# Tokens' 1/rms applied behind the input products instead of to x, seven products on two pairs of the first block, and a later fetch of x by tokens

## The chip, the cores and the metric

The kernel runs on one core of one Trainium2 chip. The metric is the device time of one launch in microseconds (us), as a median over runs; the trace is of one more execution, taken by the hardware profiler.

## The reference, cut to what matters

x has 256 tokens of 2,048 values, all in float32. h is x divided by its root mean square per token, times a gain norm_g. h times a matrix of 2,048 x 11,264 gives nine parts: q, k, v, the gate z_a (1,024 columns each), u_b, v_b, z_b (1,024 each) and g_a, g_b (2,048 each).

```python
h = rms_norm(x, norm_g)
proj = h @ w_in
q, k, v, z_a, u_b, v_b, z_b, g_a, g_b = jnp.split(proj, cuts, axis=-1)
q = rms_norm(q per head, q_norm_g); k = rms_norm(k per head, k_norm_g)
y_a = (attention(q, k, v) * silu(z_a)) @ w_proj_a
sgu = gelu(u_b) * (W_s @ rms_norm(gelu(v_b)) + b)
y_b = (sgu * silu(z_b)) @ w_proj_b
out = x + (sigmoid(g_a) * y_a + sigmoid(g_b) * y_b) @ w_out
```

The 1/rms of a token is one factor of a whole row of proj, so it can be applied to x or to the rows of proj.

## The kernel before, in words

**Precision.** Each float32 operand is split into a high half (a cast to float32r by ScalarE, names ending in h) and a low half (the difference, by VectorE, names ending in l). A product is three matmuls, lo x hi, hi x hi and hi x lo (three(), L298 to L303), each 128x128 by 128x512.

**The weight stream.** schedule() (L50) lists 120 groups; each is 1 MB of weights, fetched on SyncE's queue (load, L116) into one of four rotating buffers "raw". For an input or output block of 1,024 columns ("quad": q, k, v, za, vb, ub, zb, four g, two out) a group is one pair kp of k tiles: tile kp and tile kp + 8 of the 2,048 rows, that is a 2x2 block product. It is done in one of two ways:
- plain (direct(), L307): 8 block products, 24 matmuls into four accumulators; the weights need one cast of 2,048 columns (L125) and one difference (L126);
- seven products (seven(), L321): Strassen's scheme in Winograd's form, 21 matmuls into seven banks; the weights need combinations t (L143, L145, L146), casts whp (L152) and th (L154), differences wlp (L155) and tl (L157). t stands in a buffer of the raw rotation. The x side needs four combinations of the blocks of x, "forms" (L277 and L282), with their halves Fh and Fl (L291). At the end of the block early() (L346, a copy on ScalarE and four operations on VectorE) and final() (four more) combine the seven banks.

Pairs 0 to 3 of a block (and 4 of g) take the seven products, the others the plain way. The first block, q, is plain throughout: groups 0 to 7, pairs 0 to 7 in that order (PLAIN, L46).

**x in the first block.** xT holds x by channels, in the order of the pairs; load_x (L171) fetches k tiles p0 to p1 of it, so load_x(2, 4) is pair 1. The first piece, xv, has the small vectors and tile 0. split_x (L201) multiplies a pair by norm_g and makes the halves xuh and xul; q is computed with these, x not yet divided by its rms. Meanwhile x by tokens, xnat, is fetched (two 1 MB pieces, L187 to L190, around the fourth weight group), stats (L241) sums its squares on ScalarE, GpSimd takes the power -0.5, two transposes spread 1/rms along the free axis (stats_row, L246), VectorE multiplies x by it (normalise, L254), and halves_x (L258) makes the halves xh and xl, with which all later blocks work. q's four accumulators are copied out with 1/rms as ScalarE's scale (L690).

**The order.** Each engine runs its instructions in one order. For ScalarE and VectorE the code before L659 and the first eight passes of the loop (L658) stand inside manual_schedule (L634, closed at L660): their instructions keep the written order. In pass i the loop issues load(i + 3), split(i + 2) and split_x, then the matmuls of group i, then what at() (L572, L581 on) has put down for group i. The other engines' orders, TensorE's and the DMA queue of SyncE among them, are the scheduler's, which also may put a later instruction into a gap.

**Pools.** "big" has ten slots of 1 MB (xt0, xt1, xnat0, xnat1, xuh, xul, xh, xl, the forms and later tiles), "unit" ten of 256 KB, "raw" four, wh and wl three each, whp and wlp two each. PSUM has eight banks; a block's seven products use four banks E beside its four accumulators L, and the next block swaps the two sets. The vector gain of the spatial part (L230) is a constant tile, the spatial weights ws (L227) stand in "unit"; both are fetched by load_mix (L223), put down for the fifth block.

**After the products.** sums (L370) takes the squares of q, k and v_b per head on ScalarE, and GpSimd's power gives rs (rsqrt, L236); norm_qk and norm_v multiply by rs; func applies Silu or Gelu; turn_p (L454) transposes the attention weights and copies them out of PSUM.

Of the kernel before, what the change touches and what calls it, by code (L numbers as in the profile page):

```python
# [44 lines left out]
OUT = ((0, 1, 4, 2, 5, 3, 6, 7), (4, 0, 1, 5, 2, 3, 6, 7))  # L45
PLAIN = (0, 1, 2, 3, 4, 5, 6, 7)  # L46
NVEC = KT + 2 + H


def schedule():  # L50
    s = []

    def quad(name, c, order):
        s.extend(("quad", name, c, kp, n) for n, kp in enumerate(order))

    quad("q", 0, PLAIN)
    for name in ("k", "v", "za", "vb", "ub", "zb"):
        quad(name, 0, MIXED)
    for c in range(4):
        quad("g", c, GATE)  # L60
        s.extend(("proj", "proj", c, q, q) for q in range(4))
    for c in range(2):
        quad("out", c, OUT[c])
    return s
# [3 lines left out]
def hybrid_layer_kernel(  # L68
# [26 lines left out]
    def bank(b, name):  # L95
        return psum.tile([P, B], F32, tag=f"b{b}", name=name)
# [8 lines left out]
    def strassen(i):  # L105
        if i >= NG or G[i][0] != "quad" or G[i][1] == G[0][1]:
            return False
        return G[i][3] in SK or (G[i][1] == "g" and G[i][3] == 4)

# [71 lines left out]
    load_x(2, 4)  # L181
    load(1, pieces=2)
    load_x(4, 8)
    load(2, pieces=2)
    load_x(8, 12)
    load_x(12, 16)
    xn = [slot(F32, f"xnat{m}") for m in range(2)]  # L187
    nc.sync.dma_start(xn[0], x[0:P, :])
    load(3)
    nc.sync.dma_start(xn[1], x[P:S, :])  # L190
    for i in range(2):
# [40 lines left out]
    rstd = const.tile([P, 2], F32, name="rstd")  # L232
    R = xv[:, NVEC:]
    ssum = const.tile([P, 2], F32, name="ssum")
# [6 lines left out]
    def stats():  # L241
        for m in range(2):
            nc.scalar.activation(xn[m], xn[m], AF.Square, accum_out=ssum[:, m:m + 1])
        rsqrt(rstd, ssum, 2, D)

    def stats_row():  # L246
        ps = bank(0, "ps_R")
        for m in range(2):
            nc.tensor.transpose(ps[:, m * P:(m + 1) * P], rstd[:, m:m + 1].to_broadcast([P, P]), ident)
        nc.scalar.copy(R, ps[:, 0:S])  # L250

    xh, xl = [None, None], [None, None]

    def normalise(i):  # L254
        src = xt[i]
        nc.vector.tensor_tensor(src, src, R[:, None, :].to_broadcast([P, 8, S]), op=ALU.mult)

    def halves_x(i):  # L258
        xh[i] = slot(F32R, f"xh{i}").rearrange("p (k t) -> p k t", t=S)
        xl[i] = slot(F32R, f"xl{i}").rearrange("p (k t) -> p k t", t=S)  # L260
        nc.scalar.copy(xh[i], xt[i])
        nc.vector.tensor_tensor(xl[i], xt[i], f(xh[i]), op=ALU.subtract)

# [9 lines left out]
    def halves_4():  # L273
        nc.scalar.copy(spare(xh[0]), X["F4"])
        nc.vector.tensor_tensor(spare(xl[0]), X["F4"], f(spare(xh[0])), op=ALU.subtract)

# [92 lines left out]

    def sums(C, name):  # L370
        for m in range(2):
            for c in range(2):
                ss = small.tile([P, 4], F32, tag="ss", bufs=8, name="ss")
                junk = u("junk")
                for h in range(4):
                    nc.scalar.activation(junk[:, h * P:(h + 1) * P], C[m][c][:, h * P:(h + 1) * P], AF.Square,
                                         accum_out=ss[:, h:h + 1])
                rs = small.tile([P, 4], F32, tag="rs", bufs=8, name="rs")
                rsqrt(rs, ss, 4, P)
                X["rs", name, m, c] = rs  # L380

# [18 lines left out]
    def func(name, fn):  # L400
        for m in range(2):
            for c in range(2):
                nc.scalar.activation(X[name][m][c], X[name][m][c], fn)

# [49 lines left out]
    def turn_p(hg, banks):  # L454
        pt = X["PT", hg] = slot(F32, f"PT{hg}")[:, 0:12 * P].rearrange("p (n h t) -> p n h t", n=3, t=P)
        for n, (c, b) in enumerate(((0, 0), (1, 0), (1, 1))):
            s = X["S0", hg] if c == 0 else X["S1"][:, 4 * hg:4 * hg + 4, :]
            ps = bank(banks[n], f"ps_p{hg}{n}")
            for h in range(4):
                nc.tensor.transpose(ps[:, h * P:(h + 1) * P], s[:, h, b * P:(b + 1) * P], ident)  # L460
            nc.scalar.copy(pt[:, n], ps.rearrange("p (h t) -> p h t", t=P))

# [117 lines left out]

    i0 = first["q", 0]  # L581
    at(i0 + 1, stats)
    at(i0 + 3, stats_row)
    at(i0 + 3, normalise, 1)
    at(i0 + 4, halves_x, 1)
    at(i0 + 5, normalise, 0)
    at(i0 + 4, forms_4)
    at(i0 + 5, lambda: forms(xt[0], "x"))
    at(i0 + 6, halves_x, 0)
    at(i0 + 6, halves_f, "x")  # L590
    at(i0 + 20, halves_4)
# [48 lines left out]
    split(0, 4, [3])  # L640
    for kp in range(1, 4):
        split_x(kp)
        if kp < 2:
            split(kp, 4)
    def fac(name):
        if name == "q":
            return xu_h, xu_l
        if name == "out":
            return [X.get(("mh", i)) for i in range(2)], [X.get(("ml", i)) for i in range(2)]
        return xh, xl  # L650

# [6 lines left out]
    for i, (kind, name, c, kp, n) in enumerate(G):  # L658
        if i == 8:  # L659
            ordered.close()  # L660
        if i:
            load(i + 3)
        split(i + 2, 2 if i == 0 else 1)
        if i < 4:
            split_x(i + 4)
        plain = i < 8
        if kind == "quad":
            if n == 0:
# [4 lines left out]
                Et = None  # L673
            if len(Lt) == 3 and (plain or not strassen(i)):
                Lt.append(bank(L[3], f"acc_{name}{c}_3"))
            if strassen(i) and Et is None:
                Et = [bank(b, f"seven_{name}{c}_{j}") for j, b in enumerate(E)]
            if strassen(i):
                last = 4 if name == "g" else SK[-1]
                f8 = "m" if name == "out" else "x"  # L680
                seven(Et, Lt, i, kp, kp == SK[0], kp == last, n > 0, *fac(name), X["Fh", f8], X["Fl", f8])
                if kp == last:
                    e = early(Et, f"{name}{c}", xres.get(c) if name == "out" else None)
            else:
                direct(Lt, *fac(name), i, kp, (n == 0, not direct22(i)), n == 7)
            if n == 7:
                if plain:
                    X[name] = [[u(f"{name}{m}{j}") for j in range(2)] for m in range(2)]
                    for j in range(4):
                        nc.scalar.activation(X[name][j // 2][j % 2], Lt[j], AF.Copy, scale=rstd[:, j // 2:j // 2 + 1])  # L690
                elif name == "out":
                    post_out(c, Lt, e)
                elif name == "g":
                    X["g", c] = final(Lt, e)
                    for m in range(2):
                        for j in range(2):
                            nc.scalar.activation(X["g", c][m][j], X["g", c][m][j], AF.Sigmoid)
                else:
                    X[name] = final(Lt, e)
# [79 lines left out]
```

## Time and profile before

| | us |
|---|---|
| median of the three runs | 672.03 |
| lowest and highest | 668.34, 673.25 |
| the profiled execution, device time | 668.8 |
| its span in the trace | 667.0 |

Times in the trace are microseconds from the start of the span, durations in the page's groups nanoseconds. PE is TensorE's matmul row, PEld its weight loads, DVE VectorE, ACT ScalarE, POOL GpSimd, SP SyncE; SPq is a sequencer issuing a DMA. In the timeline a matmul's own duration (0.39 us) is longer than the step from one matmul to the next, since matmuls overlap; the starts are what counts. A bracket at the end of a line says how long the engine stood idle before it and what ended that.

### The profile page before, as it was taken

Reading aid. Unit: us, or ns where it says so; the run is one execution under the profiler, and the core shown is the slowest. Engines: PE = TensorE matmul, PEld = TensorE weight load, DVE = VectorE, ACT = ScalarE, POOL = GpSimd, SP = SyncE. Lnnn points to the kernel's source line nnn. Section 1 sums busy time; section 2 is a strip of 40 time slices with the busy share of each in tenths; the row PEclk is TensorE's granted clock in tenths of the full one; section 3 lists DMA queues with packets and bytes.
Section 4 is the critical chain, followed back from the end, with each engine's and each line's share of the span. In section 5 each row is a group of like instructions: output and inputs, shape, how many; then the busy total and the mean of one; then the engine's idle time right before and its main releaser. Section 6 shows DMA issues by size and latency. Waiting matters only on the chain.

```text
span 667.0 us, 7852 instructions
## 1 busy us (share of the span) xinstructions
PE 655.3 (98%) x2982; PEld 539.3 (81%) x2982; DVE 614.2 (92%) x605; ACT 427.0 (64%) x562; POOL 32.1 (5%) x28
## 2 busy tenths in 40 slices
PE   8899999999999999999999999999999999999997
PEld 4687788878888888888887888888888888888886
DVE  4499999899999699999999999989979989998996
ACT  7778968856995579674656845554564556746360
POOL 1000501300001004000000000000000000000000
PEclk9899999999999999999999999999999999999999
DMA  8962574455455615744545644845573474747641
GB/s 310 421 225 95 215 255 177 169 220 179 157 200 191 252 65 188 259 178 171 207 146 220 269 167 149 324 151 188 193 294 116 187 273 167 252 143 290 203 185 63
DMA packets 21925, 135.32 MB, mean 203 GB/s; under 512 B 2432, under 2 KB 3072, under 8 KB 6656
## 3 DMA queue, kind: packets, MB, share of 16 engines
q1 hardware_dynamic: 20736, 132.73, 53.8%
q10 hardware_dynamic: 1152, 2.10, 1.0%
q8 instruction: 23, 0.38, 0.2%
q14 instruction: 14, 0.11, 0.0%
HBM read 132.72 MB, written 2.10 MB: 202 GB/s over the span
## 4 chain that ended last, share of the span: by engine, by line
PE 48%; DVE 29%; ACT 8%; issue 8%; DMA 5%; POOL 1%; SPq 0%; DVEq 0%; ACTq 0%
PE acc_g L303 13%; PE y L303 11%; PE acc_out L303 9%; PE seven_g L303 6%; DVE tl L157 6%; DVE wl L126 5%; DMA raw<-in_w 5%; DVE t L143 3%; PE seven_out L303 3%; DVE wlp L155 3%; PE acc_vb L303 3%; ACT wh L125 3%; DVE t L145 2%; DVE t L146 2%; PE seven_vb L303 2%
## 5 line engine op out<-in xcount | busy, mean ns | idle before, releaser
L154 ACT CAST th<-t 128x1024 fp32r<-128x1024 f32 x104 | 109.2, 1053 | 114.5 <-DVE t L143 52.2
L126 DVE TENSOR_TENSOR wl<-raw,wh 128x2048 fp32r<-128x2048 f32 (+2 forms) x75 | 156.0, 2087 | 27.5 <-ACT wh L125 27.2
L125 ACT CAST wh<-raw 128x2048 fp32r<-128x2048 f32 (+2 forms) x75 | 130.8, 1751 | 54.8 <-PE acc_g L303 23.4
L157 DVE TENSOR_TENSOR tl<-t,th 128x1024 fp32r<-128x1024 f32 x104 | 126.1, 1217 | 3.9 <-ACT th L154 3.9
L155 DVE TENSOR_TENSOR wlp<-raw,whp 128x1536 fp32r<-128x1536 f32 x52 | 91.0, 1750 | 4.4 <-ACT whp L152 4.4
L152 ACT CAST whp<-raw 128x1536 fp32r<-128x1536 f32 x52 | 76.8, 1481 | 28.0 <-DMA raw<-in_w 13.0
L143 DVE TENSOR_TENSOR t<-raw 128x1024 f32<-128x1024 f32 x52 | 63.2, 1216 | 0.2
L303 PE MATMUL acc_g<-wh,xh 128*128 128x512 f32 x96 | 37.4, 389 | 0.0
L303 PE MATMUL acc_g<-wh,xl 128*128 128x512 f32 x96 | 37.3, 389 | 0.0
L303 PE MATMUL acc_g<-wl,xh 128*128 128x512 f32 x96 | 37.0, 389 | 0.0
L146 DVE TENSOR_TENSOR t<-t,raw 128x512 f32<-128x512 f32 x52 | 35.8, 689 | 0.3
L145 DVE TENSOR_TENSOR t<-t,raw 128x512 f32<-128x512 f32 x52 | 35.8, 689 | 0.2
L239 POOL TENSOR_TENSOR rs<-ms,mhalf 128x4 f32<-128x4 f32 x12 | 23.7, 1991 | 124.9 <-DVE ms L238 124.9
L303 PE MATMUL acc_q<-wl,xuh 128*128 128x512 f32 x64 | 26.1, 408 | 2.0 <-DVE wl L126 2.0
L303 PE MATMUL acc_q<-wh,xuh 128*128 128x512 f32 x64 | 25.6, 400 | 1.5 <-ACT wh L125 1.5
L303 PE MATMUL acc_q<-wh,xul 128*128 128x512 f32 x64 | 25.9, 404 | 0.8 <-ACT wh L125 0.8
L303 PE MATMUL y<-wh,zbl 128*128 128x512 f32 x64 | 25.1, 392 | 0.0
L303 PE MATMUL y<-wh,zal 128*128 128x512 f32 x64 | 25.0, 390 | 0.0
L303 PE MATMUL y<-wh,zah 128*128 128x512 f32 x64 | 25.0, 390 | 0.0
L303 PE MATMUL y<-wl,zah 128*128 128x512 f32 x64 | 24.9, 389 | 0.0
L303 PE MATMUL y<-wh,zbh 128*128 128x512 f32 x64 | 24.9, 389 | 0.0
L303 PE MATMUL y<-wl,zbh 128*128 128x512 f32 x64 | 24.9, 389 | 0.0
(502 smaller groups left out, 1599.9 us busy)
## 6 DMA issues: line engine op xcount, KB each, us to landing
raw<-in_w SPq DMA_DIRECT2D x117, 1024.0 KB, 4.8
raw<-in_w SPq DMA_DIRECT2D x5, 512.0 KB, 7.7
xnat<-in_x SPq DMA_DIRECT2D x2, 1024.0 KB, 12.7
xres<-in_x ACTq DMA_DIRECT2D x8, 256.0 KB, 4.9
xt<-in_xT SPq DMA_DIRECT2D x3, 512.0 KB, 9.6
out<-out_c SPq DMA_DIRECT2D x5, 256.0 KB, 2.5
raw<-in_w SPq DMA_DIRECT2D x2, 256.0 KB, 4.6
ws<-in_wsT SPq DMA_DIRECT2D x2, 256.0 KB, 2.9
```

The costliest lines, as they stand in the source:

```text
L125: nc.scalar.copy(h, r)
L126: nc.vector.tensor_tensor(l, r, f(h), op=ALU.subtract)
L143: nc.vector.tensor_tensor(two, r[:, B:3 * B].rearrange("p (a n) -> p a n", a=2), r[:, None, 0:B].to_broadcast([P, 2, B]), op=ALU.add)
L145: nc.vector.tensor_tensor(t[:, 2 * B:3 * B], t[:, 0:B], r[:, 2 * B:3 * B], op=ALU.add)
L146: nc.vector.tensor_tensor(t[:, 3 * B:], t[:, 2 * B:3 * B], r[:, 3 * B:], op=ALU.add)
L152: nc.scalar.copy(wh[i], r[:, B:])
L154: nc.scalar.copy(th[i][:, sl], t[:, sl])
L155: nc.vector.tensor_tensor(wl[i], r[:, B:], f(wh[i]), op=ALU.subtract)
L157: nc.vector.tensor_tensor(tl[i][:, sl], t[:, sl], f(th[i][:, sl]), op=ALU.subtract)
L239: nc.gpsimd.tensor_tensor(dst, ms[:, :n], mhalf[:, :n], op=ALU.pow)
L303: nc.tensor.matmul(acc, a, b, start=(start and n == 0), stop=(stop and n == 2))
```

## The change

x is no longer divided by its rms. All blocks work with xuh and xul (x times norm_g), the forms too, and 1/rms is given to ScalarE as the scale of a call behind the product: in the squares of q and k (whose rs is then multiplied by 1/rms on GpSimd), in Silu, Gelu and Sigmoid, and, for v, in the copies of the transposed attention weights. stats_row, normalise and halves_x go. Block q takes its pairs in the order FIRST and uses the seven products on pairs 2 and 3 (groups 5 and 6), so q is finished by early and final. The loads of x are put in that order, one pair between the weight groups. x by tokens is fetched by load_nat, written in pass 3 behind load(6), and stats stands in pass 6.

```diff
--- before.py
+++ after.py
@@ -43,7 +43,8 @@
 MIXED = (4, 5, 0, 1, 6, 2, 3, 7)
 GATE = (5, 0, 1, 6, 2, 3, 4, 7)
 OUT = ((0, 1, 4, 2, 5, 3, 6, 7), (4, 0, 1, 5, 2, 3, 6, 7))
-PLAIN = (0, 1, 2, 3, 4, 5, 6, 7)
+FIRST = (0, 1, 4, 5, 6, 2, 3, 7)
+FIRST_SK = (2, 3)
 NVEC = KT + 2 + H
 
 
@@ -53,7 +54,7 @@
     def quad(name, c, order):
         s.extend(("quad", name, c, kp, n) for n, kp in enumerate(order))
 
-    quad("q", 0, PLAIN)
+    quad("q", 0, FIRST)
     for name in ("k", "v", "za", "vb", "ub", "zb"):
         quad(name, 0, MIXED)
     for c in range(4):
@@ -103,8 +104,10 @@
     raw, wh, wl, th, tl = {}, {}, {}, {}, {}
 
     def strassen(i):
-        if i >= NG or G[i][0] != "quad" or G[i][1] == G[0][1]:
+        if i >= NG or G[i][0] != "quad":
             return False
+        if G[i][1] == G[0][1]:
+            return G[i][3] in FIRST_SK
         return G[i][3] in SK or (G[i][1] == "g" and G[i][3] == 4)
 
     def load_piece(i, a, b):
@@ -180,14 +183,19 @@
     load_piece(0, 2 * B, WORDS)
     load_x(2, 4)
     load(1, pieces=2)
+    load_x(8, 10)
+    load(2, pieces=2)
+    load_x(10, 12)
+    load(3, pieces=2)
+    load_x(12, 14)
     load_x(4, 8)
-    load(2, pieces=2)
-    load_x(8, 12)
-    load_x(12, 16)
-    xn = [slot(F32, f"xnat{m}") for m in range(2)]
-    nc.sync.dma_start(xn[0], x[0:P, :])
-    load(3)
-    nc.sync.dma_start(xn[1], x[P:S, :])
+    load_x(14, 16)
+
+    def load_nat():
+        X["xn"] = [slot(F32, f"xnat{m}") for m in range(2)]
+        for m in range(2):
+            nc.sync.dma_start(X["xn"][m], x[m * P:(m + 1) * P, :])
+
     for i in range(2):
         xu_h.append(slot(F32R, f"xuh{i}").rearrange("p (k t) -> p k t", t=S))
         xu_l.append(slot(F32R, f"xul{i}").rearrange("p (k t) -> p k t", t=S))
@@ -230,7 +238,6 @@
         nc.sync.dma_start(gain, bass.AP(tensor=sg.tensor, offset=sg.offset, ap=[[0, P], [1, P]]))
 
     rstd = const.tile([P, 2], F32, name="rstd")
-    R = xv[:, NVEC:]
     ssum = const.tile([P, 2], F32, name="ssum")
 
     def rsqrt(dst, src, n, count):
@@ -240,26 +247,9 @@
 
     def stats():
         for m in range(2):
-            nc.scalar.activation(xn[m], xn[m], AF.Square, accum_out=ssum[:, m:m + 1])
+            t = X["xn"][m]
+            nc.scalar.activation(t, t, AF.Square, accum_out=ssum[:, m:m + 1])
         rsqrt(rstd, ssum, 2, D)
-
-    def stats_row():
-        ps = bank(0, "ps_R")
-        for m in range(2):
-            nc.tensor.transpose(ps[:, m * P:(m + 1) * P], rstd[:, m:m + 1].to_broadcast([P, P]), ident)
-        nc.scalar.copy(R, ps[:, 0:S])
-
-    xh, xl = [None, None], [None, None]
-
-    def normalise(i):
-        src = xt[i]
-        nc.vector.tensor_tensor(src, src, R[:, None, :].to_broadcast([P, 8, S]), op=ALU.mult)
-
-    def halves_x(i):
-        xh[i] = slot(F32R, f"xh{i}").rearrange("p (k t) -> p k t", t=S)
-        xl[i] = slot(F32R, f"xl{i}").rearrange("p (k t) -> p k t", t=S)
-        nc.scalar.copy(xh[i], xt[i])
-        nc.vector.tensor_tensor(xl[i], xt[i], f(xh[i]), op=ALU.subtract)
 
     def spare(t):
 
@@ -271,8 +261,8 @@
         X["F4"] = Fs[:, :, 0]
 
     def halves_4():
-        nc.scalar.copy(spare(xh[0]), X["F4"])
-        nc.vector.tensor_tensor(spare(xl[0]), X["F4"], f(spare(xh[0])), op=ALU.subtract)
+        nc.scalar.copy(spare(xu_h[0]), X["F4"])
+        nc.vector.tensor_tensor(spare(xu_l[0]), X["F4"], f(spare(xu_h[0])), op=ALU.subtract)
 
     def forms(src, name):
         Fs = slot(F32, f"F{name}").rearrange("p (a k t) -> p a k t", a=4, t=P)
@@ -368,15 +358,20 @@
 
 
     def sums(C, name):
+
+        r = [1.0, 1.0] if name == "vb" else [rstd[:, m:m + 1] for m in range(2)]
         for m in range(2):
             for c in range(2):
                 ss = small.tile([P, 4], F32, tag="ss", bufs=8, name="ss")
                 junk = u("junk")
                 for h in range(4):
-                    nc.scalar.activation(junk[:, h * P:(h + 1) * P], C[m][c][:, h * P:(h + 1) * P], AF.Square,
+                    sl = slice(h * P, (h + 1) * P)
+                    nc.scalar.activation(junk[:, sl], C[m][c][:, sl], AF.Square, scale=r[m],
                                          accum_out=ss[:, h:h + 1])
                 rs = small.tile([P, 4], F32, tag="rs", bufs=8, name="rs")
                 rsqrt(rs, ss, 4, P)
+                if name != "vb":
+                    nc.gpsimd.tensor_scalar(rs, rs, r[m], None, op0=ALU.mult)
                 X["rs", name, m, c] = rs
 
     def norm_qk(name):
@@ -400,7 +395,7 @@
     def func(name, fn):
         for m in range(2):
             for c in range(2):
-                nc.scalar.activation(X[name][m][c], X[name][m][c], fn)
+                nc.scalar.activation(X[name][m][c], X[name][m][c], fn, scale=rstd[:, m:m + 1])
 
     def transpose4(b, src, name):
         ps = bank(b, name)
@@ -458,7 +453,7 @@
             ps = bank(banks[n], f"ps_p{hg}{n}")
             for h in range(4):
                 nc.tensor.transpose(ps[:, h * P:(h + 1) * P], s[:, h, b * P:(b + 1) * P], ident)
-            nc.scalar.copy(pt[:, n], ps.rearrange("p (h t) -> p h t", t=P))
+            nc.scalar.activation(pt[:, n], ps.rearrange("p (h t) -> p h t", t=P), AF.Copy, scale=rstd[:, b:b + 1])
 
     def attend(hg, banks):
         v, pt = X["v"], X["PT", hg]
@@ -579,15 +574,11 @@
         fn(*a, free["banks"][n0:n1])
 
     i0 = first["q", 0]
-    at(i0 + 1, stats)
-    at(i0 + 3, stats_row)
-    at(i0 + 3, normalise, 1)
-    at(i0 + 4, halves_x, 1)
-    at(i0 + 5, normalise, 0)
-    at(i0 + 4, forms_4)
-    at(i0 + 5, lambda: forms(xt[0], "x"))
-    at(i0 + 6, halves_x, 0)
-    at(i0 + 6, halves_f, "x")
+    at(i0 + 2, lambda: forms(xt[0], "x"))
+    at(i0 + 2, halves_f, "x")
+    at(i0 + 3, forms_4)
+    at(i0 + 3, load_nat)
+    at(i0 + 6, stats)
     at(i0 + 20, halves_4)
     i0 = first["k", 0]
     at(i0 + 1, sums, None, "q")
@@ -638,16 +629,13 @@
     split_x(0, [1])
     split(0, 4, [2])
     split(0, 4, [3])
-    for kp in range(1, 4):
-        split_x(kp)
-        if kp < 2:
-            split(kp, 4)
+    split_x(FIRST[1])
+    split(1, 4)
+    split_x(FIRST[2])
     def fac(name):
-        if name == "q":
-            return xu_h, xu_l
         if name == "out":
             return [X.get(("mh", i)) for i in range(2)], [X.get(("ml", i)) for i in range(2)]
-        return xh, xl
+        return xu_h, xu_l
 
     def direct22(i):
 
@@ -660,10 +648,9 @@
             ordered.close()
         if i:
             load(i + 3)
-        split(i + 2, 2 if i == 0 else 1)
-        if i < 4:
-            split_x(i + 4)
-        plain = i < 8
+        split(i + 2, 2 if i < 2 else 1)
+        for pair in {0: FIRST[3:4], 1: FIRST[4:7], 3: FIRST[7:]}.get(i, ()):
+            split_x(pair)
         if kind == "quad":
             if n == 0:
                 if i and G[i - 1][0] == "quad":
@@ -671,30 +658,28 @@
                     E, L = L, E
                 Lt = [bank(b, f"acc_{name}{c}_{j}") for j, b in enumerate(L[:3])]
                 Et = None
-            if len(Lt) == 3 and (plain or not strassen(i)):
+            if len(Lt) == 3 and not strassen(i):
                 Lt.append(bank(L[3], f"acc_{name}{c}_3"))
             if strassen(i) and Et is None:
                 Et = [bank(b, f"seven_{name}{c}_{j}") for j, b in enumerate(E)]
             if strassen(i):
-                last = 4 if name == "g" else SK[-1]
+                sk = FIRST_SK if i < 8 else SK
+                last = 4 if name == "g" else sk[-1]
                 f8 = "m" if name == "out" else "x"
-                seven(Et, Lt, i, kp, kp == SK[0], kp == last, n > 0, *fac(name), X["Fh", f8], X["Fl", f8])
+                seven(Et, Lt, i, kp, kp == sk[0], kp == last, n > 0, *fac(name), X["Fh", f8], X["Fl", f8])
                 if kp == last:
                     e = early(Et, f"{name}{c}", xres.get(c) if name == "out" else None)
             else:
                 direct(Lt, *fac(name), i, kp, (n == 0, not direct22(i)), n == 7)
             if n == 7:
-                if plain:
-                    X[name] = [[u(f"{name}{m}{j}") for j in range(2)] for m in range(2)]
-                    for j in range(4):
-                        nc.scalar.activation(X[name][j // 2][j % 2], Lt[j], AF.Copy, scale=rstd[:, j // 2:j // 2 + 1])
-                elif name == "out":
+                if name == "out":
                     post_out(c, Lt, e)
                 elif name == "g":
                     X["g", c] = final(Lt, e)
                     for m in range(2):
                         for j in range(2):
-                            nc.scalar.activation(X["g", c][m][j], X["g", c][m][j], AF.Sigmoid)
+                            nc.scalar.activation(X["g", c][m][j], X["g", c][m][j], AF.Sigmoid,
+                                                 scale=rstd[:, m:m + 1])
                 else:
                     X[name] = final(Lt, e)
         elif kind == "proj":
```

## Rows read from the trace of the kernel before

**Rows 1.** The page: busy time, share of the span and instructions of each engine.

```profile
PE 655.3 (98%) x2982; PEld 539.3 (81%) x2982; DVE 614.2 (92%) x605; ACT 427.0 (64%) x562; POOL 32.1 (5%) x28
```

**Rows 2.** Timeline, TensorE: start, duration (us), line, operation, out<-in, shapes, count [idle before].

```profile
6.22 0.50 PE L303 MATMUL acc_q<-wh,xuh 128*128 128x512 f32 x1 [1.48 <-ACT wh L125]
...
24.02 0.39 PE L303 MATMUL acc_q<-wl,xuh 128*128 128x512 f32 x1
...
27.54 0.50 PE L303 MATMUL acc_q<-wl,xuh 128*128 128x512 f32 x1 [1.59 <-DVE wl L126]
...
28.71 0.63 PE L303 MATMUL acc_q<-wh,xul 128*128 128x512 f32 x1
...
31.27 0.63 PE L303 MATMUL acc_q<-wh,xul 128*128 128x512 f32 x1
...
34.27 0.38 PE L249 MATMUL ps_R<-ident,rstd 128*128 128x128 f32 x2
...
34.72 0.40 PE L303 MATMUL acc_q<-wh,xuh 128*128 128x512 f32 x1
...
56.26 0.39 PE L303 MATMUL acc_k<-wh,xl 128*128 128x512 f32 x1
...
98.56 0.39 PE L303 MATMUL acc_v<-wh,xl 128*128 128x512 f32 x1
```

**Rows 3.** Windows, all engines: stretch, busy us (x count) of each, granted clock, DMA, GB/s.

```profile
20.00:30.00 10.00, 7.59 (x30) 5.55 (x29) 3.16 (x3) 6.71 (x7) 0.00 (x0) 0.92 1.01 418
...
28.00:30.00 2.00, 2.00 (x8) 1.52 (x7) 0.09 (x1) 2.00 (x3) 0.00 (x0) 0.60 0.99 414
```

**Rows 4.** Timeline, ScalarE.

```profile
13.15 0.91 ACT L205 ACTIVATE xt<-xt,xv 128x256 f32<-128x256 f32 x2
...
14.62 0.91 ACT L205 ACTIVATE xt<-xt,xv 128x256 f32<-128x256 f32 x2
...
23.26 1.90 ACT L125 CAST wh<-raw 128x2048 fp32r<-128x2048 f32 x1 [3.71 <-DMA raw<-in_w]
...
54.78 1.92 ACT L294 CAST Fhx<-Fx 128x2048 fp32r<-128x2048 f32 x1
...
116.47 0.99 ACT L388 ACTIVATE k_c<-k_c,rs 128x128 f32<-128x128 f32 x3 [2.19 <-POOL rs L239]
```

**Rows 5.** Timeline, VectorE.

```profile
25.19 2.29 DVE L126 TENSOR_TENSOR wl<-raw,wh 128x2048 fp32r<-128x2048 f32 x1 [4.92 <-ACT wh L125]
...
42.92 2.28 DVE L262 TENSOR_TENSOR xl<-xt,xh 128x2048 fp32r<-128x2048 f32 x1
45.13 0.28 DVE L286 TENSOR_TENSOR F<-xt 128x128 f32<-128x128 f32 x1
...
52.13 0.68 DVE L286 TENSOR_TENSOR Fx<-xt 128x512 f32<-128x512 f32 x1
...
54.66 2.28 DVE L126 TENSOR_TENSOR wl<-raw,wh 128x2048 fp32r<-128x2048 f32 x1
...
95.21 0.68 DVE L350 TENSOR_TENSOR k_h<-seven_k,k_c 128x512 f32<-128x512 f32 x1
...
107.80 1.21 DVE L143 TENSOR_TENSOR t<-raw 128x1024 f32<-128x1024 f32 x1
...
114.08 0.37 DVE L238 TENSOR_SCALAR ms<-ss 128x4 f32<-128x4 f32 x4
```

**Rows 6.** Timeline, SyncE's queue: issues of DMAs.

```profile
13.07 0.33 SPq L230 DMA_DIRECT2D gain<-in_sg  x1
14.42 34.28 SPq L111 DMA_DIRECT2D raw<-in_w  x8
...
196.44 1.64 SPq L227 DMA_DIRECT2D ws<-in_wsT  x2
```

**Rows 7.** Timeline, GpSimd.

```profile
1.54 0.29 POOL masks.py:199 TENSOR_SCALAR_AFFINE_SELECT ident<-ident 128x128 f32<-128x128 f32 x1
...
114.31 7.18 POOL L239 TENSOR_TENSOR rs<-ms,mhalf 128x4 f32<-128x4 f32 x4 [37.09 <-DVE ms L238]
```

## The prediction

> **What bounds the kernel now.** I read the page's busy shares first: TensorE is busy 98% of the span [rows 1], so time is lost only where TensorE waits or runs slowly, and a saving counts only if it removes matmuls or such waits. The matmul stream then shows where those are. Fed without a break, TensorE starts a 512-column matmul every 0.227 us: from the second matmul of the fifth group at 34.72 to the first of block k at 56.26 there are 95 steps [rows 2]. A plain group (24 matmuls) takes 5.44 us, a seven-product group (21) takes 4.76 us. Block q has 8 x 24 = 192 matmuls, 43.5 us at that step, but runs from 6.22 to 56.26, 50.0 us: 6.5 us are lost. The third group starts 23 steps before 24.02, at 18.8, so the first 48 matmuls took 12.6 us instead of 10.9: 1.7 lost at the start. The rest sits together: from 24.02 to 27.54 only three steps are made, because w3 (the fourth weight group) is late (2.8 us), then eight matmuls run 0.43 us apart (1.6 us), and two transposes for the row of 1/rms at 34.27 take 0.2 us [rows 2]. Block k has 96 + 84 = 180 matmuls, 40.8 us, and takes 98.56 - 56.26 = 42.3 us: 1.5 us lost. The windows say why w3 is late: the DMA engines are full (share 1.01, 418 GB/s in 20 to 30 us) [rows 3], and ScalarE sat idle 3.71 us until w3 landed at 23.26 [rows 4]. VectorE idled 4.92 us behind it [rows 5]. That is what the change can give: at most 6.5 + 1.5 us, plus the matmuls it removes.
>
> **Part one, the loads.** I count bytes in queue order (a weight group 1.05 MB, a k pair of x 0.26, the first x piece with vectors 0.145, a half of x by tokens 1.05). Before, w3 ends 7.35 MB and lands at 23.2. At 0.418 MB per us a piece that ends at b lands near 23.2 - (7.35 - b)/0.418. After: pair 4 ends at 2.90 (12.6 us), w2 at 3.95 (15.1), pair 5 at 4.21 (15.7), w3 at 5.26 (18.2), pair 6 at 5.52 (18.8), pairs 2 and 3 at 6.04 (20.1), pair 7 at 6.30 (20.7). w3 comes 5.0 us earlier, so the 2.8 us wait goes. What is late next is w4. If the tokens' copy really stays behind w6, w4 takes the place that w3 has now and lands at 23.2. The queue's order is the scheduler's, though: the gain vector, written in the fifth block, went out at 13.07 ahead of w4 [rows 6]. The spatial weights, written beside it but held in a rotating pool, went out only at 196.44 [rows 6]. The tokens' tiles are in such a pool, the tenth and eleventh of ten slots. So I take them as staying late; one ahead of w4 would make it 25.7, both 28.2.
>
> **Part two, ScalarE in block q.** Its order is written by hand. Scaling and halving a pair takes 14.62 - 13.15 = 1.47 us, a 2,048-column cast 1.9 [rows 4]. From 13.15: pair 4, w2, pair 5, w3, pairs 6, 2, 3 come to 5 x 1.47 + 2 x 1.9 = 11.2, so w4's cast starts at 24.3 with all its data there, and ends at 26.2. Removed are two casts of normalised halves, the copy of the row and four copies of q out of PSUM; these sit behind it and free ScalarE, which isn't the limit.
>
> **Part three, VectorE.** It loses two normalising products and two differences of 2,048 columns (2.21 each from xl to the next instruction [rows 5]): 8.8 us. It gains, for two groups, a seven-product preparation in place of a plain difference: the set from 107.80 to 114.08 is 6.28 us [rows 5], so 2 x (6.28 - 2.21) = 8.1; and eight combinations of q out of PSUM (0.68 each, about 0.62 in a row by the Fx rows [rows 5]): 5.0. Net +4.3 us on the second busiest engine, set against idle time of some 9 us around w3 and w4 in the present head. What decides is where it stands. In written order from w4's cast: difference w4 26.2 to 28.4; four forms Fx, 54.66 - 52.13 = 2.53 [rows 5], to 30.9; then VectorE waits for ScalarE's cast of Fx (1.92, row Fhx [rows 4]) until 32.8; Fl to 35.1; preparation of pair 2 to 41.3; pair 7's difference and the forms of pair 4 (0.6 + 0.9: four of 0.28 [rows 5], overlapped) to 42.9; preparation of pair 3 to 49.2; w7 to 51.4; k's first group to 53.6; q's four early combinations to 56.0. ScalarE's two sums of squares and a cast hold k's second group until 60.0; q's last four combinations to 62.5; k's first two preparations to 68.8 and 75.1.
>
> **Part four, TensorE.** Six matmuls go (1.36 us), and the two transposes. The third group ends at 24.24 as now. w3 is ready at 21.5, w4 at 28.4, so two plain groups run without a break to 35.1. From there TensorE alone would need 4.76 + 4.76 + 5.44 and end at 50.1, 6.2 us before now. VectorE doesn't allow it: the last low halves of pair 3 are there at 49.2, w7's at 51.4. In strict order pair 3's third matmul waits for its first low half at 46.9 (49.2 less two differences of 1.14), 19 follow, 51.2, and the plain group ends at 56.6. With high-half products drawn forward it ends at 49.7 + 5.44 = 55.1, and never below 51.4 + 8 x 0.227 = 53.2. I take 55.5, since in block k the order on TensorE isn't the written one either: 0.8 us gained of the 6.2. In k, from 55.5, the plain groups need 55.5 and 60.9 (halves ready at 53.6 and 60.0), the seven-product groups start at 66.4 and 71.2 and want their last halves about 4 us later (68.8, 75.1). I put k's loss at 0.5 instead of 1.5: 1.0 gained. Bounds for k: 0 to 1.5 gained.
>
> **Part five, the rest.** 1/rms as ScalarE's scale replaces unscaled calls one for one: nothing. GpSimd gets eight multiplications of 128x4 for q and k. No row shows one: 0.29 us is the 128x128 select, 2 us the 128x4 power [rows 7]. I take 0.3, nearest in kind, and keep 2. ScalarE waited 2.19 us for the power in k [rows 4], so 0.3 lengthens that wait little; the turned q and k are needed much later.
>
> **Sum.** -0.8 - 1.0 = -1.8 us. The profiled execution took 668.8 us (span 667.0), so 667.0 by it; it is 3.2 us below the median of the runs, so on the median 672.03 - 1.8 = 670.2 us.
>
> **A clock rule.** The trace shows the granted clock at 0.60 in 28 to 30 us [rows 3], that is, some time at 1.2 GHz instead of 2.4, right after the stretch with two matmuls in 3.3 us, and 1.6 us lost by it [rows 2]. The Trainium skill (TensorE: Matmul & The Clock Gate, Part 1, What's actually happening) says that the throttled state is the default and that activity releases it. The trace agrees, and by that rule the change could meet the drop again, later: it is the second rival below.
>
> **Rivals.** (1) Slower: both halves of x by tokens go out ahead of w4. It lands at 28.2 rather than before 24.3, and everything on VectorE's chain moves by 3.9: -1.8 + 3.9 = +2.1, 674.1. It decides from w4 landing after 26.1, where the gain is spent. For it: the gain vector's place; against it: the spatial weights'. One half only: +1.4, 671.6, inside the forecast. (2) The clock: in strict order TensorE has two matmuls between 35.6 and 39.0 and again between 42.5 and 46.9, much like before 27.54. Eight slow matmuls after the second hole end block q at 56.6 + 1.6 = 58.2, 1.9 later than now; k then loses nothing, so +0.4, 672.4. (3) VectorE doesn't hold TensorE up: q ends at 50.1 and k loses nothing, -6.2 - 1.5 = -7.7, 664.3. For it: w3's and the clock's losses are gone; against it: the 23 us of written work from 28.4 to 51.4. (4) GpSimd's multiplications cost 2 us, so each group of 1/rms comes at half the rate, and ScalarE stands before the scalings of q and k with casts queued behind them. That is 8 x (2 - 0.3) = 13.6 us of waiting; ScalarE is busy 64% [rows 1], so by an estimate some 9 of them push work back: -1.8 + 9 = +7, 679.2. It decides from about 0.8 us a piece. For it: the 2.19 us wait is there already; against it: power is a costlier operation than a product, and the selects are short [rows 7]. The Trainium skill (GPSIMD Engine Reference, 2.1 Instruction dispatch) gives about 6 us for a first call of freshly loaded code; no row here shows that, and by it the sum would be about +2.
>
> **How the numbers follow.** Forecast with one half of x early 0.52, clock 0.20, x ahead of w4 0.15, TensorE unhindered 0.08, GpSimd 0.05. About 1% (6.7 us) is what a measurement of this kernel can tell from no change. Faster by that only in (3) and in a little of the forecast's upper end: 0.10; slower in (4) and where (1) and (2) come together: 0.07; within it 0.83. The present runs spread from 668.3 to 673.3, so the range goes from (3), just inside, to (1) with 2 us of spread: 664 to 676.
>
> **What would show it.** Right: w3's cast near 18 to 20 us, no wait of TensorE at 24 to 27, waits for wl, wlp or tl in 35 to 51 instead, VectorE without a break from 33, block k starting at 53 to 57. Wrong: tokens' DMA ahead of w4 (1); a granted clock under 1 in 36 to 52 (2); k starting near 50 (3); long waits of ScalarE for GpSimd's rs (4).

## The result, and the profile after

The changed kernel takes 676.2 us (median of 9 runs, 674.8 to 677.8) where the one before took 672.3: ratio 1.0085, interval 1.0058 to 1.0111. The forecast was 670.2. The profiled execution has a span of 673.8 us, 6.8 more than before. By the medians it is 3.9, since the profiled execution of the kernel before, 668.8 us, is one of its short ones (its runs go from 668.3 to 673.3). The first matmul of each block, from the views of the blocks' tiles, says where the time goes:

| first matmul of | before | after | difference |
|---|---|---|---|
| v | 98.6 | 104.3 | +5.7 |
| za | 142.0 | 149.2 | +7.2 |
| vb | 190.4 | 197.2 | +6.8 |
| y (first projection) | 368.3 | 374.7 | +6.4 |
| out | 580.9 | 587.3 | +6.4 |

All of it arises before za. Block q isn't the place: its last matmul starts at 55.9 (56.0 before), and two matmuls of k already run at 51.8. The loss is in k and, to a smaller part, in v.

The timeline of TensorE in the changed kernel:

```profile
45.40 0.50 PE L293 MATMUL seven_q<-th,Flx 128*128 128x512 f32 x1 [1.70 <-ACT th L157]
...
83.33 0.39 PE L293 MATMUL seven_k<-wlp,xuh 128*128 128x512 f32 x1
...
86.51 0.50 PE L293 MATMUL seven_k<-th,Flx 128*128 128x512 f32 x1 [2.80 <-ACT th L157]
...
90.88 0.50 PE L293 MATMUL seven_k<-th,Flx 128*128 128x512 f32 x1 [1.91 <-ACT th L157]
...
92.89 0.63 PE L293 MATMUL acc_k<-whp,Flx 128*128 128x512 f32 x1
...
95.02 0.63 PE L293 MATMUL seven_k<-whp,xul 128*128 128x512 f32 x1
```

The hole at 24 to 27 us of [rows 2] is gone; new ones stand at 83 and 88, both ended by a cast th on ScalarE, and behind them the matmuls from 92.89 to 95.02 run 0.43 us apart. The windows (columns as in [rows 3]) show the lower clock there, and the full one in 44 to 50 us of block q:

```profile
44.00:50.00 6.00, 3.92 (x15) 2.77 (x16) 5.96 (x7) 4.86 (x4) 0.00 (x0) 1.00 0.43 142
...
80.00:90.00 10.00, 5.64 (x23) 3.71 (x21) 3.48 (x5) 7.43 (x19) 5.35 (x8) 1.00 0.11 45
90.00:96.00 6.00, 5.12 (x15) 4.05 (x16) 6.00 (x6) 3.58 (x3) 0.00 (x0) 0.72 0.38 105
```

From 80 to 90 VectorE is busy only 3.48 of 10 us: the second busiest engine waits too. Its timeline, then ScalarE's and GpSimd's:

```profile
28.13 0.69 DVE L276 TENSOR_TENSOR Fx<-xt 128x512 f32<-128x512 f32 x1
...
32.72 2.29 DVE L285 TENSOR_TENSOR Flx<-Fx,Fhx 128x2048 fp32r<-128x2048 f32 x1 [1.98 <-ACT Fhx L284]
...
43.00 1.22 DVE L146 TENSOR_TENSOR t<-raw 128x1024 f32<-128x1024 f32 x1
...
50.01 4.49 DVE L129 TENSOR_TENSOR wl<-raw,wh 128x2048 fp32r<-128x2048 f32 x2
...
73.23 0.38 DVE L245 TENSOR_SCALAR ms<-ss 128x4 f32<-128x4 f32 x4
73.52 2.28 DVE L129 TENSOR_TENSOR wl<-raw,wh 128x2048 fp32r<-128x2048 f32 x1
...
79.66 0.68 DVE L148 TENSOR_TENSOR t<-t,raw 128x512 f32<-128x512 f32 x1
86.49 1.23 DVE L160 TENSOR_TENSOR tl<-t,th 128x1024 fp32r<-128x1024 f32 x1 [6.15 <-ACT th L157]
```

```profile
23.98 1.91 ACT L128 CAST wh<-raw 128x2048 fp32r<-128x2048 f32 x1
...
82.52 2.58 ACT L383 ACTIVATE q_c<-q_c,rs 128x128 f32<-128x128 f32 x8 [6.90 <-POOL rs L374]
85.12 0.40 ACT L383 ACTIVATE q_h<-q_h,rs 128x128 f32<-128x128 f32 x1
85.43 1.03 ACT L157 CAST th<-t 128x1024 fp32r<-128x1024 f32 x1
...
125.69 0.40 ACT L383 ACTIVATE k_c<-k_c,rs 128x128 f32<-128x128 f32 x1 [2.64 <-POOL rs L374]
```

```profile
73.47 7.74 POOL L246 TENSOR_TENSOR rs<-ms,mhalf 128x4 f32<-128x4 f32 x1 [11.67 <-DVE ms L245]
81.19 1.00 POOL L246 TENSOR_TENSOR rs<-ms,mhalf 128x4 f32<-128x4 f32 x1
82.19 0.30 POOL L374 TENSOR_SCALAR rs<-rs,rstd 128x4 f32<-128x4 f32 x1
82.46 1.03 POOL L246 TENSOR_TENSOR rs<-ms,mhalf 128x4 f32<-128x4 f32 x1
...
122.53 4.34 POOL L374 TENSOR_SCALAR rs<-rs,rstd 128x4 f32<-128x4 f32 x2
```

Read from the bottom: GpSimd runs two powers and then the first product, and the first power alone takes 7.74 us; ScalarE's next instruction, the scaling of q, stands 6.90 us for the first rs ([rows 4] had 2.19 as its longest); the cast th behind it in ScalarE's queue comes at 85.43; VectorE, which needs it, idles 6.15 us; TensorE runs dry. In that idle time a power takes 1.00 to 1.03 us and a product 0.30, the power at 82.46 while TensorE and ScalarE are at work.

The slow power begins beside VectorE's difference wl and ends at 81.21, 0.87 us after VectorE's row of instructions without a gap has ended (79.66 + 0.68 = 80.34). That row ended because VectorE lacked the cast th that stands behind ScalarE's wait: here the wait ended only when it had starved VectorE.

The queue of SyncE shows x by tokens behind w4 to w6, as taken:

```profile
13.53 4.60 SPq L114 DMA_DIRECT2D raw<-in_w  x3
18.18 0.42 SPq L238 DMA_DIRECT2D gain<-in_sg  x1
18.65 12.48 SPq L197 DMA_DIRECT2D xnat<-in_x  x2
```

### The profile page after: what moved, and what is told of

The parts are those of the page before. It is cut to its first block, busy times and chain, and to the rows that moved or that the text cites. A ratio compares the mean times of both kernels' runs of the same rounds, so it can differ in the third digit from the quotient of the medians.

```text
span 673.8 us, 7863 instructions
## 1 busy us (share of the span) xinstructions
PE 655.9 (97%) x2974; PEld 539.0 (80%) x2974; DVE 618.6 (92%) x620; ACT 430.6 (64%) x561; POOL 43.0 (6%) x36
## 4 chain that ended last, share of the span: by engine, by line
PE 65%; DVE 20%; issue 5%; ACT 5%; POOL 2%; DMA 2%; SPq 0%; DVEq 0%; ACTq 0%
PE acc_g L293 13%; PE y L293 11%; PE acc_out L293 9%; PE seven_g L293 6%; DVE tl L160 5%; PE acc_za L293 4%; PE acc_vb L293 4%; PE acc_ub L293 4%; PE seven_out L293 3%; DVE wl L129 3%; DVE t L146 3%; DVE wlp L158 2%; POOL rs L246 2%; DMA raw<-in_w 2%; ACT wh L128 2%
## 5 line engine op out<-in xcount | busy, mean ns | idle before, releaser
L157 ACT CAST th<-t 128x1024 fp32r<-128x1024 f32 x108 | 113.1, 1052 | 112.9 <-DVE t L146 52.3
L129 DVE TENSOR_TENSOR wl<-raw,wh 128x2048 fp32r<-128x2048 f32 (+2 forms) x74 | 151.5, 2056 | 19.2 <-ACT wh L128 19.1
L128 ACT CAST wh<-raw 128x2048 fp32r<-128x2048 f32 (+2 forms) x74 | 127.0, 1725 | 48.6 <-PE acc_g L293 21.5
L160 DVE TENSOR_TENSOR tl<-t,th 128x1024 fp32r<-128x1024 f32 x108 | 131.1, 1220 | 10.2 <-ACT th L157 10.2
L293 PE MATMUL acc_g<-wh,xul 128*128 128x512 f32 x96 | 37.4, 389 | 0.0
L293 PE MATMUL acc_g<-wh,xuh 128*128 128x512 f32 x96 | 37.4, 389 | 0.0
L293 PE MATMUL acc_g<-wl,xuh 128*128 128x512 f32 x96 | 37.0, 389 | 0.0
L293 PE MATMUL acc_out<-wl,mh 128*128 128x512 f32 x64 | 24.9, 389 | 0.0
L293 PE MATMUL acc_out<-wh,mh 128*128 128x512 f32 x64 | 24.9, 389 | 0.0
L293 PE MATMUL acc_out<-wh,ml 128*128 128x512 f32 x64 | 24.9, 389 | 0.0
```

The lines of the kernel that those rows point to most:

```text
L128: nc.scalar.copy(h, r)
L129: nc.vector.tensor_tensor(l, r, f(h), op=ALU.subtract)
L157: nc.scalar.copy(th[i][:, sl], t[:, sl])
L160: nc.vector.tensor_tensor(tl[i][:, sl], t[:, sl], f(th[i][:, sl]), op=ALU.subtract)
L293: nc.tensor.matmul(acc, a, b, start=(start and n == 0), stop=(stop and n == 2))
```

## The experiments

Theory A: ScalarE's wait for GpSimd makes the loss. Theory B: the two seven-product groups give VectorE too much. Each ratio is against the kernel before on the same chip; the span and the starts are those of one profiled execution.

| run | ratio (interval) | span | first of v | first of za |
|---|---|---|---|---|
| the change | 1.0085 (1.0058 to 1.0111) | 673.8 | 104.3 | 149.2 |
| e1_folded_eps | 0.9998 (0.9968 to 1.0028) | 669.1 | 101.9 | 144.6 |
| e2_no_wait_for_power | 0.9925 (0.9901 to 0.9949) | 665.1 | 97.8 | 140.4 |
| e3_plain_q | 0.9896 (0.9851 to 0.9940) | 663.0 | 94.0 | 136.5 |
| e4_before_with_product | 1.0048 (1.0022 to 1.0074) | 671.5 | 101.4 | 146.5 |
| e5_plain_q_folded | 0.9884 (0.9846 to 0.9922) | 663.1 | 93.9 | 136.5 |
| e6_plain_q_early_tokens | 0.9982 (0.9961 to 1.0002) | 667.3 | 99.2 | 141.8 |
| e8_one_pair_seven | 1.0024 (0.9999 to 1.0049) | 671.1 | 101.6 | 145.9 |
| e9_one_pair_no_wait | 0.9871 (0.9833 to 0.9909) | 660.6 | 93.3 | 135.9 |
| e10_one_pair_folded | 0.9947 (0.9923 to 0.9970) | 665.1 | 96.8 | 140.6 |
| e11_one_pair_scalar_power | 0.9983 (0.9960 to 1.0005) | 666.8 | 95.6 | 142.3 |
| e12_two_pairs_scalar_power | 1.0023 (0.9997 to 1.0050) | 669.7 | 98.9 | 144.5 |

**e1**, no multiplication on GpSimd:

```diff
-nc.scalar.activation(junk[:, sl], C[m][c][:, sl], AF.Square, scale=r[m], ...)
+nc.scalar.activation(junk[:, sl], C[m][c][:, sl], AF.Square, ...)
-rsqrt(rs, ss, 4, P); nc.gpsimd.tensor_scalar(rs, rs, r[m], None, op0=ALU.mult)
+rsqrt(rs, ss, 4, P, eps=ssum[:, m:m + 1])   # ssum * EPS / D + EPS * EPS
```

> The changed kernel without GpSimd's eight multiplications and with plain squares: rs = (mean(q^2) + eps * (mean(x^2) + eps)) ^ -0.5, which is the same value, with the token's eps as VectorE's second scalar. The first rs then needs one power instead of two powers and a product. Theory A (ScalarE's queue stands at the scaling of q by rs until GpSimd delivers, and the casts th behind it starve VectorE and TensorE): the wait of 6.9 us before that scaling falls to 2 to 5 us, and the time by 2 to 5 us, 671 to 674 us. Theory B (VectorE has too much to do since block q has seven products on two pairs): no change, 675 to 677 us.

ScalarE's wait fell from 6.9 to 4.8 us in q and went in k; the time fell by 0.9%, a little more than A expected, and B's no change is refuted. The first rs came after one power of 1.01 us, but now the second power was the slow one (6.97 us), and ScalarE waited for it after four scalings. The edit also takes the scale out of 32 squares, each of which gets 0.09 us shorter (0.39 to 0.30), so not all of the gain is the wait's.

**e2**, the same instructions in the same order on TensorE, VectorE, ScalarE and GpSimd, only without that wait:

```diff
-X["rs", name, m, c] = rs
+X["rs", name, m, c] = rs if name == "vb" else ms
```

> The changed kernel with q and k scaled by VectorE's ms (mean of squares plus eps) instead of rs. It leaves the power -0.5 and the factor 1/rms out of the normalisation of q and k; GpSimd computes rs as before, but nobody waits for it. ScalarE's order stays the same. Theory A: the 6.9 us and 2.6 us waits go, block k takes about 42 us instead of 48 and v 43 instead of 45, the time falls by 6 to 8 us, 668 to 670 us. Theory B: VectorE's backlog stays, 675 to 677 us.

1.0085 - 0.9925 is 1.6%, 10.8 us (8.7 by the spans): the wait is more than the whole loss. GpSimd's own timeline got worse meanwhile, since VectorE no longer paused. Its first power took 9.48 us and ended at 82.64, again 0.87 us after the first gap between VectorE's instructions (at 81.77, of 0.03 us):

```profile
73.16 9.48 POOL L246 TENSOR_TENSOR rs<-ms,mhalf 128x4 f32<-128x4 f32 x1 [11.66 <-DVE ms L245]
82.61 1.28 POOL L246 TENSOR_TENSOR rs<-ms,mhalf 128x4 f32<-128x4 f32 x1
83.89 2.03 POOL L375 TENSOR_SCALAR rs<-rs,rstd 128x4 f32<-128x4 f32 x1
```

**e3**, seven products in q undone (and q copied out of PSUM unscaled):

```diff
 if G[i][1] == G[0][1]:
-    return G[i][3] in FIRST_SK
+    return False
```

> The changed kernel with block q plain throughout (six matmuls more, 1.4 us; two preparations by VectorE and eight combinations less, 13 us). Theory A: the scaling of q still waits for GpSimd, the time stays within 2 us of 676 us. Theory B: VectorE keeps up and the time falls by 5 us or more, under 671 us.

This is B's number, and A's was wrong: the wait doesn't stay. With q plain the first two powers take 1.46 and 1.01 us, and ScalarE comes to the scaling only after them. VectorE is busy there too, 2.32 of 2.50 us, but with gaps between its instructions. GpSimd, the window, then ScalarE:

```profile
59.76 2.43 POOL L246 TENSOR_TENSOR rs<-ms,mhalf 128x4 f32<-128x4 f32 x2 [9.87 <-DVE ms L245]
62.18 1.75 POOL L374 TENSOR_SCALAR rs<-rs,rstd 128x4 f32<-128x4 f32 x2
```

```profile
59.70:62.20 2.50, 2.50 (x12) 2.07 (x12) 2.32 (x4) 2.50 (x8) 2.44 (x3) 1.00 0.85 344
```

```profile
67.52 1.28 ACT L383 ACTIVATE q<-q,rs 128x128 f32<-128x128 f32 x4
```

So undoing the seven products takes the wait away as well, and e3 alone can't part A from B. In its trace x by tokens also goes out later, at 28.95 us instead of 18.65.

**e4**, the kernel before with such a product:

```diff
 rsqrt(rs, ss, 4, P)
+if name != "vb": nc.gpsimd.tensor_scalar(rs, rs, mhalf[:, m:m + 1], -2.0, op0=ALU.mult, op1=ALU.mult)
```

> The kernel before with one product more on GpSimd behind each power of q and k (rs times 1, 128x4). Theory A: the first rs comes later by a power and a product, ScalarE's waits of 1.0 and 2.2 us grow to 3 to 7 us, and the time goes up by 2 to 5 us, 674 to 677 us. Theory B: no change, 671 to 673 us.

The time went up by 0.48%, 3.2 us, with waits of 3.1 and 4.8 us for GpSimd (1.0 and 2.2 before). A's mechanism works in the old kernel too.

**e5**, e1 and e3 together:

> Both edits at once: block q plain throughout, and 1/rms folded into the eps of q's and k's normalisation, so that GpSimd has no multiplication. With q plain, ScalarE waited only 0.6 and 0.4 us for GpSimd, so both theories say little is left to gain: 0 to 1 us below the kernel with q plain (ratio to the kernel before 0.988 to 0.991, 662 to 665 us where the kernel before takes 670).

As expected; it can't be told from e3.

**e6**, e3 with the tokens where the kernel before fetches them. The edit also moves load(3), the fourth weight group w3, behind three loads of x, as in the kernel before, so it tests the order of the loads as a whole:

```diff
+load_x(12, 14); load_x(4, 8); load_x(14, 16)
+nc.sync.dma_start(X["xn"][0], x[0:P, :])
 load(3, pieces=2)
+nc.sync.dma_start(X["xn"][1], x[P:S, :])
...
-at(i0 + 3, load_nat)
```

> Block q plain, and x by tokens fetched where the kernel before has it (one half ahead of the fourth weight group, one behind it) instead of behind the seventh. If the 3 us by which block q ends sooner come from the order of the loads, the wait for the fourth group and the drop of the clock behind it come back: q ends at 55 to 57 us and the time is 3 to 5 us above the kernel with q plain (667 to 669 us where that takes 664). If they come from the work that VectorE lost (products and halves of the normalised x), q ends at 53 us and the time stays.

The last matmul of q starts at 58.2 instead of 53.0, and 0.86% are lost, 5.8 us: somewhat more than expected on both counts. ScalarE waits 4.18 us for w3 again, and behind it come more waits of TensorE and the drop of the clock (0.83 granted in 40 to 50 us). ScalarE, then TensorE:

```profile
21.68 2.25 ACT L128 CAST wh<-raw 128x1024 fp32r<-128x1024 f32 x2 [4.18 <-DMA raw<-in_w]
```

```profile
38.82 0.50 PE L296 MATMUL acc_q<-wh,xul 128*128 128x512 f32 x1 [0.98 <-ACT wh L128]
41.55 0.80 PE L296 MATMUL acc_q<-wl,xuh 128*128 128x512 f32 x1 [1.53 <-DVE wl L129]
```

Without the new order of the loads the rest of e3 is worth 0.2%, and that interval includes no change.

**e7**, the probe (one run, 663.9 us):

```diff
+def probe(n, src=None):
+    t = xv[:, NVEC:NVEC + 4]
+    for j in range(n):
+        nc.gpsimd.tensor_scalar(t, t if src is None or j else X[src][0][0][:, 0:4], mhalf[:, 0:1], -2.0, ...)
```

> The kernel with q plain, with products of 128x4 on GpSimd that nobody waits for: 6 near the start, where VectorE does little, and 24 in a row in the second block of g, where VectorE is busy over 95%. Theory C (a small GpSimd instruction has to wait out VectorE's running one): 0.3 us each at the start, 1 us or more each in g, with more of it where VectorE's instructions are long. If the durations are GpSimd's own: 0.3 us in both places. The time stays within 2 us of the kernel with q plain.

The products in three stretches: the number, shortest/median/longest in ns, and the first and last start. Then the longest product, VectorE's timeline beside it and where its work changes, and the windows of the last two stretches:

```profile
L222 POOL TENSOR_SCALAR xv<-xv,mhalf x6: 270/270/438, 3.7 to 6.1; 128x4 f32<-128x4 f32 x6
L222 POOL TENSOR_SCALAR xv<-xv,mhalf x15: 273/2174/3445, 390.3 to 418.9; 128x4 f32<-128x4 f32 x15
L222 POOL TENSOR_SCALAR xv<-xv,mhalf x8: 270/270/272, 421.2 to 423.8; 128x4 f32<-128x4 f32 x8
```

```profile
394.11 3.44 POOL L222 TENSOR_SCALAR xv<-xv,mhalf 128x4 f32<-128x4 f32 x1
```

```profile
394.07 2.29 DVE L129 TENSOR_TENSOR wl<-raw,wh 128x2048 fp32r<-128x2048 f32 x1 [0.56 <-ACT wh L128]
396.28 1.22 DVE L160 TENSOR_TENSOR tl<-t,th 128x1024 fp32r<-128x1024 f32 x1
...
418.70 2.28 DVE L129 TENSOR_TENSOR wl<-raw,wh 128x2048 fp32r<-128x2048 f32 x1
420.94 0.69 DVE L345 TENSOR_TENSOR g_h<-seven_g,g_c 128x512 f32<-128x512 f32 x1
```

```profile
389.00:421.00 32.00, 32.00 (x143) 26.50 (x142) 31.37 (x28) 17.77 (x14) 30.60 (x16) 1.00 0.56 201
421.00:424.00 3.00, 3.00 (x15) 2.49 (x14) 2.93 (x5) 2.21 (x2) 2.25 (x9) 1.00 1.03 421
```

At the start, where VectorE does little, a product takes 0.27 us (one 0.44). In the block of g it takes 2.17 us at the median up to 421 us, and 0.27 again behind that, though VectorE and TensorE are full in both windows (VectorE 31.37 of 32 and 2.93 of 3). What differs is the kind of VectorE's work: up to 421 its instructions are those on the weights (t, wlp, wl, tl), with both inputs in SBUF, and from 420.94 on the combinations of the banks, with one input in PSUM. So theory C holds beside the first kind only. There nearly every product ends 0.05 to 0.15 us behind the end of one of VectorE's instructions, but often not of the first: the one of 3.44 us starts at 394.11 and ends behind the second (tl, at 397.50).

**e8**, FIRST_SK = (3,):

> The changed kernel with seven products on one pair of block q (pair 3) instead of two. Theory B (VectorE's work for the seven products delays k and starves GpSimd): between the kernel with q plain and the changed one, nearer to the changed one because the combinations of the banks stay: ratio to the kernel before 0.996 to 1.006, with a wait of ScalarE for GpSimd of 2 to 6 us. If only the wait for GpSimd counts and it is a matter of the order of instructions: anything, but the wait and the time go together (time about 667 plus the wait).

The ratio is in the expected range, but the wait is 7.0 us (2 to 6 were expected), as long as with two pairs, and the time is 4 us lower. So the time doesn't follow the wait alone.

**e9**, e8 with the edit of e2:

> Seven products on one pair of block q, and q and k scaled by VectorE's ms instead of rs (power and 1/rms left out of the normalisation of q and k), so that ScalarE doesn't wait for GpSimd. This gives the price of the seven products without that wait. Known ratios to the kernel before: q plain 0.990, two pairs without the wait 0.9925. If VectorE's work alone costs what the two pairs cost there, one pair lies between, 0.989 to 0.993 (662 to 665 us where the kernel before takes 670), and the wait is worth 1.0024 minus that, some 7 to 9 us. If it stays near 1.002, the wait isn't what makes one pair slow.

0.9871: the wait is worth 1.5%, 10 us, with one pair as with two. Without it one pair is not slower than q plain (0.9896, the intervals overlap); the second pair costs 0.0054, 3.6 us. The intervals of e2 and e9 touch, but the three other pairs of runs whose edits differ by the second pair alone say the same (0.0061, 0.0051 and 0.0040 with the change and e8, e1 and e10, e12 and e11). The cost arises in block q: its last matmul starts at 55.9 to 57.3 us with two pairs, where TensorE waits some 3 us for casts th, and at 52.1 to 52.7 with one, where it doesn't. So B is right for the second pair only.

**e10**, e8 with the edit of e1:

> Seven products on one pair of block q, with 1/rms folded into the eps (no multiplication on GpSimd, same values). VectorE is as full as with the changed kernel when the powers start, so the first power takes 3 to 6 us instead of 1 and ScalarE waits that long: ratio 0.993 to 1.000, above q plain (0.990). If the folding frees the path, 0.989 to 0.991, and the seven products would be worth keeping.

Inside the range; ScalarE still waits 4.8 us, and the slow power takes 6.97 us as in e1.

**e11** and **e12**, the power on ScalarE:

```diff
-rsqrt(rs, ss, 4, P, r[m])
+for m in range(2):
+    nc.scalar.activation(r4[:, 8 * m:8 * m + 8], s4[:, 8 * m:8 * m + 8], AF.Ln, bias=r[m], scale=1.0 / P)
+nc.scalar.activation(r4, r4, AF.Exp, scale=-0.5)
```

> Seven products on one pair of block q, 1/rms folded into the eps, and the power -0.5 of q and k on ScalarE itself, as exp(-0.5 ln(.)): two logarithms of 128x8, one exponential of 128x16 and two loads of function tables for each of q and k, all ahead of the scaling in ScalarE's own queue. Nobody waits for GpSimd in q and k; the same values are computed. By the theory that the wait is what costs, it comes near the run without the wait (0.987): four table loads of 1.3 us and the small calls are some 6 us of ScalarE, half of them in its idle time, so 0.987 to 0.993. If the wait were only a sign of a path that is long anyway, it would stay at the folded kernel's 0.995 or above.

> The same with seven products on both pairs, as in the change. Known: two pairs without the wait 0.9925, two pairs folded 0.9998. By the theory of the wait 0.992 to 0.998, and slower than one pair by about 0.5%, which is VectorE's part of the price.

Both missed: no wait for GpSimd is left, but ScalarE itself comes late. In e11 its timeline has

```profile
62.90 1.28 ACT L381 ACT_TABLE_LOAD   x1
64.20 0.49 ACT L381 ACTIVATE rs<-ss,ssum 128x8 f32<-128x8 f32 x2
64.71 1.28 ACT L382 ACT_TABLE_LOAD   x1
66.00 0.22 ACT L382 ACTIVATE rs<-rs 128x16 f32<-128x16 f32 x1
```

These four lines are 3.3 us ahead of the scalings and a cast th, the same comes again in k, and VectorE waits 4.4 us for casts; the clock also fell once, in v (0.91 granted in 120 to 140 us). By the expectation of e11, a ratio of 0.995 or above speaks for a path that is long anyway. That ScalarE's queue is the cause in all of these runs, whichever instruction stands in it, fits them, but for e11 and e12 it is argued and no run takes it apart.

The best of these that compute the whole layer are e5 and e3, at 0.9884 and 0.9896 below both kernels.

## Why the prediction was wrong

**The loads and ScalarE** were right: w4's cast was put at 24.3 and starts at 23.98; x by tokens goes out behind w6. That the new order of the loads gains is shown by e6 against e3.

**VectorE in block q** was right to within a microsecond: Fx at 28.4 (28.13), Fl at 32.8 (32.72), preparation of pair 3 at 42.9 (43.0), w7 at 49.2 (50.01, since the halves of pair 4's forms slipped in ahead). The end of q was near too: the next block was put at 55.5, and the last matmul of q starts at 55.9. But the holes between 36 and 48 us are ended by casts th of ScalarE, not by VectorE's low halves as the forecast had it. Block k was to lose 0.5 us and lost some 7.5 (48.4 us from 55.9 to 104.3, where 180 matmuls need 40.8). Without ScalarE's wait the spans show -1.9 us (e2: 665.1 against 667.0; by the medians 0.75%, 5 us). That this meets the sum of -1.8 is luck: in e2 the last matmul of q starts 1.1 us later than before, where 0.8 were to be gained.

**The step that failed** is part five: "I take 0.3 ... so 0.3 lengthens that wait little". It kept the power and the wait as the rows before have them and sized only the product. The product does take 0.30 us with VectorE idle, but it wasn't what to size. The runs showed three other things: the power beside VectorE's row without a gap took 7.74 us, not the 2 us of [rows 7]; a second power (1.00 us) stood ahead of the first product, because all four ms arrive together; and ScalarE's scaling has casts th behind it, on which VectorE and TensorE live. The wait went from 1.0 and 2.2 us to 6.9 and 2.6, and e2 prices it at 10.8 us. In the kernel before the powers ran beside a busy VectorE as well and took 1.2 to 2.8 us; why the one in the changed kernel passes over the ends of four of VectorE's instructions, no run shows.

Part five also put 1/rms as a scale at nothing. A square of q or k takes 0.39 us with it and 0.30 without, a 128x512 function 0.71 instead of 0.63. With 32 calls of each that is, by an estimate from these durations, some 6 us of ScalarE's time; what it adds to the loss no run prices.

**Rival (4)** had the place right, and its chance of 0.05 was too low. It was sized by the cost of a product and not by GpSimd's chain. Rival (1) didn't happen; rival (2)'s clock fell at 92 and not in block q, behind the hole that rival (4) made, but in e2, with the same order, it did fall in block q (0.82 granted in 44 to 50 us); rival (3) isn't what the runs without the wait show with two pairs, though e9 came to 660.6 us of span with one pair.

**Part three** counted +4.3 us of VectorE's work as bearable by its idle time. With one pair that holds (e9); the second pair costs 3.6 us more than its three matmuls give back.

## What to carry to other kernels

An instruction that waits on a slow engine costs what stands behind it in its own queue, so size the whole chain up to it (how many instructions of the slow engine, in which order) and not the one that is added. Price GpSimd's small instructions from rows in which VectorE does the same kind of work, as densely, as it will; its busy share alone doesn't tell. A change that closes VectorE's gaps can slow GpSimd and starve VectorE in turn; here the new order of the loads was worth 0.9% with q plain, and the seven products, with the wait that came with them, took more than that back.

## What the runs showed of the hardware

GpSimd's 128x4 product takes 0.27 to 0.30 us beside an idle VectorE, 2.17 us at the median beside VectorE's instructions on the weights, and 0.27 us beside its combinations of the banks (e7, VectorE full in both). The 128x4 power takes 1.00 to 1.03 us while VectorE idles, mostly 1 to 3 us beside a busy one, and 7.74 (the change) and 9.48 us (e2) beside a row of VectorE's work without a gap. These two, and the slow powers of e1, e8, e9 and e10, ended 0.87 us after the first gap in that row. The Trainium skill (GPSIMD Engine Reference, 1. Specifications) says that GpSimd's SBUF interfaces are shared with VectorE and contend with its instructions of two SBUF inputs; these numbers agree: VectorE's differences are such instructions, and the combinations of the banks, with one input in PSUM, are not. Its opposite, VectorE slowed by GpSimd, isn't seen: a 2,048-column difference took 2.29 us within the probe, 2.28 us in [rows 5].

The granted clock was 0.72 in 90 to 96 us of the changed kernel, behind holes of 2.80 and 1.91 us, and 1.00 in 44 to 50 us, behind one of 1.70. In e2, with the same instructions in the same order, it was 0.82 in 44 to 50 us. What parts the two executions no run shows.

```profile
44.00:50.00 6.00, 4.00 (x12) 2.90 (x13) 5.96 (x8) 4.95 (x4) 0.00 (x0) 0.82 0.44 153
```
